# Hybrid MLA and RWKV-7 trunk: eight block copies per inversion move from VectorE to GpSimd

## Chip, cores and metric

The kernel runs on one core of one Trainium2 chip. The metric is device time in microseconds, the median of several executions, lower being better. Every profile is one execution recorded by the hardware profiler; TensorE (PE) is the matrix engine, VectorE (DVE), ScalarE (ACT) and GpSimd (POOL) are the elementwise engines, and SyncE (SP) issues the DMAs.

## What is computed

A decoder trunk of two layers on a sequence of 1024 tokens, model width 1024, in float32. Layer 0 mixes the tokens by latent attention (12 heads), layer 1 by the RWKV-7 recurrence (24 heads of 64); each layer also has four heads of attention to a memory of 256 tokens, a SiLU gate and an output projection. The change lies in layer 1, whose recurrence is, for every head,

```
def step(state, inp):
    r_t, w_t, k_t, v_t, kk_t, a_t = inp
    sa = jnp.einsum('bhvk,bhk->bhv', state, -kk_t)
    state = (state * w_t[:, :, None, :]
             + sa[..., None] * (kk_t * a_t)[:, :, None, :]
             + v_t[..., None] * k_t[:, :, None, :])
    return state, jnp.einsum('bhvk,bhk->bhv', state, r_t)
```

The kernel does not run this token by token. It cuts the 1024 steps into chunks of 64 and solves the dependence inside a chunk with the inverse of a unit triangular 64x64 matrix for each chunk and head.

## The kernel before, in words

**Large products.** Every projection is an fp32 product done as three passes of rounded halves (`mm3`, L160 to L162). Its weights are loaded by SP (L151), rounded by ACT (`wh`, L152), and the remainder is taken by DVE (`wl`, L153, a subtraction of two SBUF operands). PE alternates these products with the small products of the recurrence.

**Layer 1 as a pipeline.** The work is 24 items: 12 pairs of heads times 2 halves of the sequence. An item goes through five stages, one stage per step, so that in each step five items are in flight: `project` (L871), `prep` (L976), `invert` (L1109), `scan` (L1191) and `norm` (L1248). The function `interleave` (L62) mixes the generators of one step; output projections, gates and the memory heads are added to some of the steps.

**The stage `invert`.** For one item it inverts sixteen 64x64 triangular matrices (8 chunks, 2 heads). Both 32x32 diagonal blocks are inverted on DVE by 31 pairs of instructions (L1136 a product into `tmp`, L1140 an addition into `U`, both with two SBUF operands). PE transposes the result into PSUM (L1148), ACT copies it into `inv` as `Uc[0]` and `Uc[1]` (L1152, four copies of 32x256). Then come the lines of the change. DVE makes `X1`, the 32x32 transposes of `Uc[0]` (L1156). Four DVE copies (L1158, 32x128 each) put the blocks of `Uc[1]` on the diagonal of `U2`, and four more (L1165, 32x256 each) put the two diagonal blocks into `XT`. PE multiplies the lower block with `X1` (L1171), ACT takes the result to `M1` (L1180), PE multiplies `M1` with `U2` (L1185), and ACT writes the off-diagonal block into `XT` (L1188). `U2` is one tile for all items, there are two `XT` tiles.

**Who uses the result.** `scan` of that item, in the next step, goes through the eight chunks. For each, DVE masks a product (`gm`, L1216), PE applies the inverse (L1218, reads `XT`), DVE copies the result (L1219), PE forms the state update (L1221) and the output (L1225), and DVE adds up the new state (L1233). The stage `prep` of the item behind has the only regular GpSimd work of layer 1, two memsets of 64x512 per item (L1066).

**What sets the order.** Every engine works through its own queue in order. The order inside a queue is fixed when the program is built: a planner of the tile framework goes by the program's order, by its own model of durations and by which buffers are free. So the queue's order need not be the program's: in some items `X1` stands after the copies on DVE although the program has it first. The tiles `X1`, `M1`, `inv` and most others come from one ring of 54 buffers of 128x512.

Of the kernel before, what the change touches and what calls it, by code (L numbers as in the profile page):

```python
# [71 lines left out]
class Build:  # L72
# [1036 lines left out]
    def invert(self, d, env):  # L1109

        XT, U2, inv, sysd = (d[x] for x in ("XT", "U2", "inv", "sysd"))
        A21 = inv[0:32]
        ip, b_tile = env["ip"], env["b_tile"]
        nc = self.nc
        mm = nc.tensor.matmul
        V, G, ACT = nc.vector, nc.gpsimd, nc.scalar
        As = ip.tile([P, 32, 32], F32, tag="As", name=self.name("As"))
        nc.sync.dma_start(
            As[:].rearrange("p a b -> p (a b)"),
            sysd[:].rearrange("b s r t -> (b s) (r t)").unsqueeze(1).broadcast_to([32, 4, 1024]),  # L1120
        )
        U = ip.tile([P, 32, 8], F32, tag="U", name=self.name("U"))
        tmp = ip.tile([P, 32, 8], F32, tag="tmp", name=self.name("tmp"))
        E = V
        if d["hf"] == 1:
            c0 = self.smp.tile([P, P], F32, tag="c0", bufs=2, name=self.name("c0"))
            nc.sync.dma_start(c0[:], self.carry[d["p"]][:])
            ACT.activation(c0[:], c0[:], AF.Copy, scale=d["f"][:, 8:9])
            d["c0"] = c0[:]
        nc.sync.dma_start(U[:].rearrange("p a b -> p (a b)"), self.A["cst"][:, CU : CU + 256])  # L1130
        for u in range(31, 0, -1):
            if u % 4 == 0:
                yield
            i0 = u // 4
            n = 8 - i0
            E.tensor_tensor(  # L1136
                out=tmp[:, 0:u, 0:n], in0=As[:, 0:u, u : u + 1].broadcast_to([P, u, n]),
                in1=U[:, u : u + 1, i0:8].broadcast_to([P, u, n]), op=ALU.mult,
            )
            E.tensor_tensor(out=U[:, 0:u, i0:8], in0=U[:, 0:u, i0:8], in1=tmp[:, 0:u, 0:n], op=ALU.add)  # L1140
        yield

        Uc = [inv[32:64], inv[64:96]]
        for ih in range(2):
            yield
            ps = b_tile()
            for i in range(4):
                nc.tensor.transpose(ps[0:32, i * P : i * P + P], U[:, :, ih * 4 + i], self.ident)  # L1148
            for b in range(2):
                src = ps[0:32, :].rearrange("p (i s c) -> p i s c", i=4, c=4)[:, :, b * 16 : b * 16 + 16, :]  # L1150
                dst = Uc[b][:, :, ih * 16 : ih * 16 + 16].rearrange("p s (i c) -> p i s c", c=4)
                ACT.copy(dst, src)  # L1152
        yield

        X1 = self.g([32, 16, 32], s="X1")
        V.transpose(X1[:].rearrange("p a b -> p (a b)"), Uc[0].rearrange("p a b -> p (a b)"))  # L1156
        for q in range(4):
            V.tensor_copy(  # L1158
                U2[32 * q : 32 * q + 32, :, 32 * q : 32 * q + 32],
                Uc[1].rearrange("p (g q) t -> p g q t", q=4)[:, :, q, :],  # L1160
            )
        for hd in range(2):
            r0 = hd * 64
            for b in range(2):
                V.tensor_copy(  # L1165
                    XT[r0 + 32 * b : r0 + 32 * b + 32, 0:8, 32 * b : 32 * b + 32],
                    Uc[b].rearrange("p (c h) t -> p c h t", h=2)[:, :, hd, :],
                )
        ps = b_tile()
        for g4 in range(4):  # L1170
            mm(  # L1171
                ps[:, g4 * P : g4 * P + P],
                A21[:, 4 * g4 : 4 * g4 + 4, :].rearrange("p s t -> p (s t)"),
                X1[:, 4 * g4 : 4 * g4 + 4, :].rearrange("p s t -> p (s t)"),
                start=True, stop=True,
            )
        yield
        M1 = self.g([P, 4, 32], s="M1")
        for q in range(4):
            ACT.copy(  # L1180
                M1[32 * q : 32 * q + 32], ps[32 * q : 32 * q + 32, :].rearrange("p (g f) -> p g f", f=P)[:, :, 32 * q : 32 * q + 32]
            )
        ps = b_tile()
        for g4 in range(4):
            mm(ps[0:32, g4 * P : g4 * P + P], M1[:, g4, :], U2[:, g4, :], start=True, stop=True)  # L1185
        for hd in range(2):
            src = ps[0:32, :].rearrange("p (c h t) -> p c h t", h=2, t=32)
            ACT.copy(XT[hd * 64 : hd * 64 + 32, 0:8, 32:64], src[:, :, hd, :])  # L1188
# [187 lines left out]
```

## Time and profile before

| | |
|---|---|
| median of 3 runs | 2519.84 us (2515.22 to 2521.16) |
| the profiled execution | 2510.56 us |
| its span | 2508.8 us |
| mean granted TensorE clock | 0.996 |
| PE busy | 2420.2 us (96%) |
| DVE busy | 1936.4 us (77%) |
| ACT busy | 1375.7 us (55%) |
| POOL busy | 55.1 us (2%) |

The busy time of PE comes from modelled ends of pipelined products. Line numbers (L1165) are those of the kernel printed above. "Idle before" is the time for which an engine had nothing running ahead of the instruction, and the name behind the arrow is what ended it. The first inversion's blocks are ready near 1099 us and the last one's near 2413 us, so that everything the change touches lies between these two times.

### The profile page before, as it was taken

How to read it: one execution, taken by the hardware profiler on the slowest of the kernel's cores; microseconds unless marked ns; L12 is line 12 of the kernel's file. 1: busy time of each engine (PE TensorE's matmuls, PEld its weight loads, DVE VectorE, ACT ScalarE, POOL GpSimd, SP SyncE). 2: the span in 40 equal slices, each digit the busy share in tenths (PEclk: the TensorE clock that was granted, in tenths of full speed). 3: DMA queues.
4: the chain of work that ended last, by engine and by line, in shares of the span. 5: the costliest groups of instructions: out<-in, count | busy, mean ns of one | idle time of the engine just before them, and what ended most of it. 6: DMA issues, size and time to landing. Idle time of an engine off the chain costs nothing.

```text
span 2508.8 us, 39875 instructions
## 1 busy us (share of the span) xinstructions
PE 2420.2 (96%) x13298; PEld 1996.1 (80%) x13298; DVE 1936.4 (77%) x5750; ACT 1375.7 (55%) x2973; POOL 55.1 (2%) x158
## 2 busy tenths in 40 slices
PE   8899999999999999999999999999999999999997
PEld 6698888888888778877778777777777777788785
DVE  7756455877787766698888888888888898786975
ACT  6445345554555334565665666666666665654542
POOL 0000000000000100000000000000000000000000
PEclk9999999999999999999999999999999999999998
DMA  5352222111112443422122222322222123222332
GB/s 178 111 171 85 76 80 74 51 56 54 49 64 68 159 168 136 143 78 76 58 73 79 80 79 78 100 82 77 79 81 80 62 84 118 87 94 98 118 137 70
DMA packets 165982, 231.45 MB, mean 92 GB/s; under 512 B 46096, under 2 KB 67984, under 8 KB 165776
## 3 DMA queue, kind: packets, MB, share of 16 engines
q1 hardware_dynamic: 165776, 228.90, 27.7%
q8 instruction: 105, 1.72, 0.3%
q14 instruction: 101, 0.83, 0.1%
HBM read 187.66 MB, written 37.49 MB: 90 GB/s over the span
## 4 chain that ended last, share of the span: by engine, by line
PE 75%; DVE 15%; ACT 6%; issue 3%; DMA 2%; SPq 0%; DVEq 0%; ACTq 0%
PE mm L160 15%; PE mm L161 15%; PE mm L162 15%; PE a L1085 3%; PE c L1218 2%; DVE tmp L1136 2%; PE pt L724 2%; DVE U L1140 2%; PE c L1221 1%; PE y L1225 1%; PE po L160 1%; PE po L161 1%; PE y L1224 1%; DVE wl L153 1%; PE po L162 1%
## 5 line engine op out<-in xcount | busy, mean ns | idle before, releaser
L152 ACT CAST wh<-wr 128x512 fp32r<-128x512 f32 (+3 forms) x500 | 299.0, 600 | 436.0 <-PE mm L161 381.0
L153 DVE TENSOR_TENSOR wl<-wr,wh 128x512 fp32r<-128x512 f32 (+3 forms) x500 | 329.6, 661 | 132.3 <-ACT wh L152 113.0
L160 PE MATMUL mm<-xnh,wh 128*128 128x512 f32 x912 | 373.9, 410 | 0.8 <-DVE qml L134 0.6
L161 PE MATMUL mm<-xnl,wh 128*128 128x512 f32 x912 | 371.2, 407 | 0.0
L162 PE MATMUL mm<-xnh,wl 128*128 128x512 f32 x912 | 369.7, 406 | 0.0
L160 PE MATMUL mm<-yh,wh 128*128 128x512 f32 x492 | 198.9, 404 | 4.3 <-DVE xr L389 4.1
L162 PE MATMUL mm<-yh,wl 128*128 128x512 f32 x492 | 196.8, 400 | 0.0
L160 PEld LDWEIGHTS mm<-xnh,wh 128*128 128x128 f32 x912 | 172.1, 189 | 30.5 <-issue 2.6
L161 PE MATMUL mm<-yl,wh 128*128 128x512 f32 x492 | 195.5, 397 | 0.0
L161 PEld LDWEIGHTS mm<-xnl,wh 128*128 128x128 f32 x912 | 172.3, 189 | 27.2 <-issue 1.4
L162 PEld LDWEIGHTS mm<-xnh,wl 128*128 128x128 f32 x912 | 172.1, 189 | 27.3 <-issue 1.0
L160 PE MATMUL mm<-xh,wh 128*128 128x512 f32 x416 | 165.2, 398 | 7.6 <-ACT xh L438 7.6
L161 PE MATMUL mm<-xl,wh 128*128 128x512 f32 x416 | 164.9, 396 | 0.6 <-DVE xl L439 0.6
L1140 DVE TENSOR_TENSOR U<-U,tmp 128x60 f32<-128x60 f32 (+24 forms) x744 | 155.9, 210 | 12.3 <-PE b L1171 0.5
L1136 DVE TENSOR_TENSOR tmp<-As,U 128x60 f32<-128x60 f32 (+24 forms) x744 | 155.6, 209 | 12.1
L162 PE MATMUL mm<-xh,wl 128*128 128x512 f32 x416 | 164.3, 395 | 0.0
L1232 ACT ACTIVATE sc<-S,f 128x128 f32<-128x128 f32 x168 | 67.4, 401 | 169.5 <-DVE S L1233 155.9
L302 ACT ACTIVATE p<-b,sm 128x512 f32<-128x512 f32 (+2 forms) x144 | 82.8, 579 | 107.3 <-DVE sm L299 82.2
L389 DVE TENSOR_TENSOR xr<-mm,xr 128x512 f32<-128x512 f32 x123 | 84.5, 688 | 67.1 <-PE mm L162 65.2
L160 PEld LDWEIGHTS mm<-yh,wh 128*128 128x128 f32 x492 | 92.7, 188 | 22.6 <-DVE xr L389 3.5
L297 DVE TENSOR_REDUCE sm<-b 128x1 f32<-128x256 f32 (+1 forms) x176 | 90.3, 527 | 24.8 <-PE b L686 10.1
L162 PEld LDWEIGHTS mm<-yh,wl 128*128 128x128 f32 x492 | 92.7, 188 | 17.0 <-issue 0.2
(361 smaller groups left out, 5968.8 us busy)
## 6 DMA issues: line engine op xcount, KB each, us to landing
wr<-in_wu_dram SPq DMA_DIRECT2D x292, 256.0 KB, 2.7
wr<-in_wo_dram SPq DMA_DIRECT2D x122, 256.0 KB, 2.6
yr<-y SPq DMA_DIRECT2D x60, 256.0 KB, 3.8
As<-sysd SPq DMA_DIRECT2D x24, 512.0 KB, 4.3
y<-y SPq DMA_DIRECT2D x32, 256.0 KB, 2.0
y<-sg SPq DMA_DIRECT2D x32, 256.0 KB, 2.0
g<-u SPq DMA_DIRECT2D x24, 256.0 KB, 2.3
gt<-g SPq DMA_DIRECT2D x24, 256.0 KB, 2.8
```

The source lines that it names most:

```text
L152: nc.scalar.copy(hi[:, :n], raw[:, :n])
L153: nc.vector.tensor_sub(lo[:, :n], raw[:, :n], hi[:, :n].bitcast(F32))
L160: mm(ps, a[0], b[0], start=start, stop=False)
L161: mm(ps, a[0], b[1], start=False, stop=False)
L162: mm(ps, a[1], b[0], start=False, stop=stop)
L297: nc.vector.tensor_reduce(sm[:, i : i + 1], ps[:, :own], AX.X, ALU.max, negate=True)
L302: nc.scalar.activation(p[:, :own], ps[:, :own], AF.Exp, bias=sm[:, 0:1], accum_out=sm[:, 2 + i : 3 + i])
L389: nc.vector.tensor_add(xs[m][:], ps[:], xs[m][:])
L1085: mm(ps[:, j * 256 : j * 256 + 256], BK[c // 4][:, c % 4, :], AR[:, c, :], start=True, stop=True)
L1136: E.tensor_tensor(out=tmp[:, 0:u, 0:n], in0=As[:, 0:u, u : u + 1].broadcast_to([P, u, n]), in1=U[:, u : u + 1, i0:8].broadcast_to([P, u, n ...
L1140: E.tensor_tensor(out=U[:, 0:u, i0:8], in0=U[:, 0:u, i0:8], in1=tmp[:, 0:u, 0:n], op=ALU.add)
L1232: ACT.activation(sc[:], cur, AF.Copy, scale=fc)
```

## The change

The four copies into `U2` and the four into `XT` are issued on GpSimd; operands, shapes and program order stay the same. `X1`, the two products and the ACT copies are as before.

```
@@ -1155,14 +1155,14 @@
         X1 = self.g([32, 16, 32], s="X1")
         V.transpose(X1[:].rearrange("p a b -> p (a b)"), Uc[0].rearrange("p a b -> p (a b)"))
         for q in range(4):
-            V.tensor_copy(
+            G.tensor_copy(
                 U2[32 * q : 32 * q + 32, :, 32 * q : 32 * q + 32],
                 Uc[1].rearrange("p (g q) t -> p g q t", q=4)[:, :, q, :],
             )
         for hd in range(2):
             r0 = hd * 64
             for b in range(2):
-                V.tensor_copy(
+                G.tensor_copy(
                     XT[r0 + 32 * b : r0 + 32 * b + 32, 0:8, 32 * b : 32 * b + 32],
                     Uc[b].rearrange("p (c h) t -> p c h t", h=2)[:, :, hd, :],
                 )
```

## Rows read from the trace of the kernel before

**Rows 1.** The page: busy time of each engine, and the chain that ended last.

```profile
PE 2420.2 (96%) x13298; PEld 1996.1 (80%) x13298; DVE 1936.4 (77%) x5750; ACT 1375.7 (55%) x2973; POOL 55.1 (2%) x158
...
PE 75%; DVE 15%; ACT 6%; issue 3%; DMA 2%; SPq 0%; DVEq 0%; ACTq 0%
```

**Rows 2.** Busy time of each engine by stretch, in layer 1.

```profile
core 0: us, PE busy (x) PEld busy (x) DVE busy (x) ACT busy (x) POOL busy (x), PEclk, DMA share, GB/s
...
1160.00:1770.00 610.00, 589.97 (x3301) 479.14 (x3300) 520.57 (x1815) 382.56 (x841) 10.26 (x20) 1.00 0.25 80
1770.00:2420.00 650.00, 630.78 (x3510) 513.56 (x3509) 547.33 (x1884) 383.51 (x846) 10.41 (x20) 1.00 0.29 96
```

**Rows 3.** Groups by line on DVE, 1100 to 2420: busy us, mean ns | idle before.

```profile
L1165 DVE COPY XT<-inv 32x256 f32<-32x256 f32 x96 | 27.6, 287 | 7.6 <-ACT inv L1152 6.1
...
L1158 DVE COPY U<-inv 32x128 f32<-32x128 f32 x96 | 20.9, 218 | 1.8
L1156 DVE STREAM_TRANSPOSE X<-inv 32x512 f32<-32x512 f32 x24 | 16.8, 700 | 10.7 <-ACT inv L1152 10.2
```

**Rows 4.** Groups by line on PE, 1100 to 2420, same columns.

```profile
L1218 PE MATMUL c<-gm,XT 128*128 128x128 f32 x368 | 74.9, 285 | 9.4 <-DVE gm L1216 3.7 <-DVE tmp L1136 2.6 <-DVE m L193 1.8
...
L334 PE MATMUL a<-cst,mp 128*128 128x128 f32 x64 | 12.0, 282 | 3.5 <-ACT mp L302 3.3
```

**Rows 5.** Timeline of DVE, 1236 to 1244: start, us, instruction [idle before <-releaser].

```profile
1236.81 0.70 DVE L1156 STREAM_TRANSPOSE X<-inv 32x512 f32<-32x512 f32 x1 [1.30 <-ACT inv L1152]
1237.54 0.91 DVE L1158 COPY U<-inv 32x128 f32<-32x128 f32 x4
1238.48 1.18 DVE L1165 COPY XT<-inv 32x256 f32<-32x256 f32 x4
1239.69 0.69 DVE L153 TENSOR_TENSOR wl<-wr,wh 128x512 fp32r<-128x512 f32 x1
...
1243.71 0.28 DVE L1216 TENSOR_TENSOR gm<-c,cst 128x128 f32<-128x128 f32 x1
```

**Rows 6.** Timeline of PE, 1237 to 1245.

```profile
1237.65 1.12 PE L1171 MATMUL b<-X,inv 32*128 32x128 f32 x8 [0.55 <-DVE X L1156]
...
1239.93 1.06 PE L1185 MATMUL b<-U,M 128*32 128x128 f32 x8
...
1244.14 0.46 PE L1218 MATMUL c<-gm,XT 128*128 128x128 f32 x2 [0.64 <-DVE tmp L1136]
```

**Rows 7.** Timeline of DVE, 1779 to 1791, an item in a step with a memory head.

```profile
1779.26 0.58 DVE L1165 COPY XT<-inv 32x256 f32<-32x256 f32 x2 [1.48 <-ACT inv L1152]
...
1781.93 0.45 DVE L1158 COPY U<-inv 32x128 f32<-32x128 f32 x2
1782.39 0.58 DVE L1165 COPY XT<-inv 32x256 f32<-32x256 f32 x2
...
1790.48 0.70 DVE L1156 STREAM_TRANSPOSE X<-inv 32x512 f32<-32x512 f32 x1
```

**Rows 8.** Groups by line on POOL, shapes kept apart: busy us, mean ns | idle before.

```profile
L728 POOL MEMSET pth<- 128x128 f32 x48 | 10.6, 221 | 762.8 <-PE mm L161 397.6 <-PE b L682 134.3 <-PE po L161 69.4
...
L807 POOL MEMSET XT<- 128x576 f32 x2 | 1.4, 717 | 0.0
...
L807 POOL MEMSET U<- 128x512 f32 x1 | 0.5, 524 | 0.0
L552 POOL TENSOR_SCALAR_AFFINE_SELECT msk<-msk 128x128 bf16<-128x128 bf16 x1 | 0.3, 293 | 0.1
```

**Rows 9.** Timeline of POOL at two places.

```profile
1101.51 0.61 POOL L1066 MEMSET SAV<- 64x512 f32 x1 [11.63 <-DMA U<-in_cst_dram]
...
1879.47 0.52 POOL L1066 MEMSET SAV<- 64x512 f32 x1 [32.02 <-PE y L1225]
```

**Rows 10.** Timeline of DVE at the same two places.

```profile
1101.08 1.49 DVE L1165 COPY XT<-inv 32x256 f32<-32x256 f32 x4
...
1879.62 0.68 DVE L1087 TENSOR_TENSOR AM<-a,cst 128x512 f32<-128x512 f32 x1
```

More of the change, by code (lines that the diff above doesn't have):

```diff
@@ L1157, in invert @@
         for q in range(4):
-            V.tensor_copy(
+            G.tensor_copy(
                 U2[32 * q : 32 * q + 32, :, 32 * q : 32 * q + 32],
@@ L1164, in invert @@
             for b in range(2):
-                V.tensor_copy(
+                G.tensor_copy(
                     XT[r0 + 32 * b : r0 + 32 * b + 32, 0:8, 32 * b : 32 * b + 32],
```

## The prediction

> **What bounds the kernel now.** I read the page first: PE is busy for 96% of the span and DVE for 77%, and the chain that ended last is 75% PE and 15% DVE [rows 1]. So the kernel is PE's, with places where PE waits for another engine, and only these places can be gained. The table of stretches says how much they hold where the change works: from 1160 to 2420 us PE is idle for (610 - 590) + (650 - 631) = 39 us of 1260, while DVE is busy for 85% [rows 2]. The groups on PE say which waits stand near the eight copies: 9.4 us ahead of L1218, which waits for DVE's mask `gm`, and 3.5 us ahead of L334 in the memory heads, which waits for ACT's exponential and through it for DVE [rows 4].
>
> The timeline of DVE shows how the copies come into this. An item's `X1` starts as the last block of `inv` arrives, U2's and XT's copies follow, then `wl`, the inversion of the next item, and only at 1243.71 the mask that PE needs at 1244.14, where PE has stood for 0.64 us [rows 5, 6]. This pattern, `X1` first and the copies right behind it, stands in 14 of the 24 items. In nine of them PE waits at L1218 within the next twenty microseconds, for 0.55 to 1.33 us, 7.2 of the 9.4 us. In the other 10 items the copies come early and `X1` three to eleven microseconds after the first of them [rows 7]; seven of these have the wait at L334.
>
> **What goes.** DVE loses 96 copies of 218 ns and 96 of 287 ns, 20.9 + 27.6 = 48.5 us of its busy time [rows 3]. In its queue one item's eight take 1239.69 - 1237.54 = 2.15 us [rows 5]. That is not 24 x 2.15 off the kernel: PE can only take back what it idles. Taken alone, 2.15 us earlier masks cover each of the nine waits whole, 7.2 us. In the rows of the memory heads, a pair of U2's copies and a pair of XT's (0.45 + 0.58 = 1.03 us) stand ahead of the maxima and products of the softmax [rows 7]; that covers the waits at L334, 3.5 us. `X1` and with it L1171 gain nothing: `X1` is ahead of the copies and waits for ACT [rows 3, 5]. The full prize is 10.7 us.
>
> **What comes: the price on POOL.** No row shows a copy on POOL. From below it costs what POOL's memset does: 221 ns for 128 elements, and, by the slope from there to 512 elements, (524 - 221) / 384 = 0.79 ns each, 322 ns for 256 [rows 8]; an item then takes 4 x (0.221 + 0.322) = 2.17 us. A gain below that has no ground, since a copy writes as much as a memset. From above I take rows for larger tiles, 524 ns for U2 and 717 ns for XT, 4.96 us. The nearest row is POOL's one instruction that reads as well as writes, the selection on 128 elements at 293 ns [rows 8]. I take 293 ns for U2's copies and 293 + 128 x 0.79 = 394 ns for XT's: 2.75 us per item, 66 us in all on an engine that is busy for 55 us of 2509 [rows 1].
>
> **What waits for them.** POOL is behind no one: the copies can start with `X1`, as the last ACT block lands. U2 must be ready by L1185, 3.12 us after `X1`'s start [rows 5, 6]; four copies take 1.2 us, at the upper price 2.1. XT must be ready by the next L1218; in the item of the rows that is 7.3 us after `X1`'s start, in the tightest of the 14 it is 5.9 us, against 2.75 (4.96 at the upper price). If that cover were gone, PE would stand at L1185 with the large products queued behind it, one microsecond for one. POOL's queue also holds two memsets per item, which fall tens of microseconds from the copies except in the first item; a memset that starts two microseconds later holds up nobody near it, as the rows it clears are first filled by the scan a step later. No DMA is issued by what moves, so SP's queue, the weights and the loads of `U` and `As` keep their order. I cost all of this at nothing.
>
> **What comes: POOL beside DVE.** This decides. The four XT copies that ran beside a memset took 1.49 us in place of 1.18, and the memset 0.61 in place of 0.52 [rows 5, 9, 10]: the two held each other up. A two-operand instruction beside a memset took 0.68 us, the time of that shape with POOL quiet [rows 5, 9, 10]. DVE's copies take (287 - 218) / 128 = 0.54 ns per element [rows 3], so they move two elements in the time in which others move about one: two streams in and two out. A memset only writes. What fits is that the engines share DVE's second path into and out of memory: a memset takes the second write path, which a two-operand instruction does not need. A copy on POOL also reads, and the second read path is what `wl`, `tmp` and `U` use for their second operand. Those are what DVE runs after `X1`. So I take it that while POOL copies, DVE's two-operand instructions stand, and the reverse. `X1`, with one operand at 700 ns for 512 elements [rows 3], runs freely and covers 1237.54 - 1236.81 = 0.73 us of the copies. The rest, 2.75 - 0.73 = 2.02 us, DVE loses; it saved 2.15. The net is 0.13 us per item, over nine waits 1.2 us. From the waits at L334 I take half, 1.7 us, since the early copies meet two-operand instructions of the memory head as well. **The sum is 1.2 + 1.7 = 2.9 us, about 3 us less.** Against the profiled execution that is 2510.56 - 3 = 2507.6 us. This execution lies 9.3 us under the median of the runs shown; taken from the median, 2519.84 - 3 gives 2517.
>
> The Trainium skill, "SBUF — State Buffer", section "Who interferes with whom", says that a VectorE instruction with two SBUF inputs contends with a GpSimd instruction that reads SBUF and not with one that only writes. The trace agrees with the second half (0.68 us beside the memset); no run here shows the first. By that rule the sum stays at 3 us; were it not so, it would be 10.7.
>
> **The rivals.**
>
> *Only the fast form collides (22%).* If a POOL copy holds up only DVE's two-stream copies, which is all that a row shows, nothing is lost to it: 7.2 + 3.5 = 10.7 us less, 2509; every wait of the two groups, 12.9, would give 2507. For it: the two-operand row beside the memset. Against it: that memset reads nothing.
>
> *POOL's copies are slow (20%).* At 524 and 717 ns DVE stands for 4.96 - 0.73 = 4.23 us per item where it saved 2.15. The loss of 2.08 us lands at L1218 in the nine items where PE already waits: 19 us more, 2539. In all 14 it would be 29 us, 2549. It decides where eight copies exceed 2.15 + 0.73 = 2.88 us, so my own price lies only just under the point. For it: 32 partitions in strips of 32 elements are a finer pattern than a memset's row. Against it: 293 ns for 128 elements read and written.
>
> The Trainium skill, "GPSIMD Engine Reference", section 3.1, calls GpSimd about half as fast as VectorE on elementwise work; doubling the 218 and 287 ns of DVE gives an estimate of 4.0 us per item and about 10 us more. Its section 4.1 calls one-input work roughly line rate, so that page of the Trainium skill speaks for both sides; no run here shows either.
>
> *The planner's new order (13%).* With DVE 2 us lighter per item the planner can place `X1`, `gm` and `wl` elsewhere. That it does so for small reasons is seen in the 10 items where `X1` went behind the copies [rows 5, 7]. The price is of the size of what stands at L1218, 9.4 us, either way [rows 4].
>
> That the change would not do what it says is no rival: the engine is named in each call.
>
> **How the numbers follow.** The forecast, collision and nearly even exchange, has 45%; its own range runs from 6.4 + 3.5 = 9.9 us less (price from below: 4 x 0.543 - 0.73 = 1.44 lost, 0.71 gained in nine waits) to 6 us more (200 ns more for each U2 copy with its XT copy, 0.8 us per item: 9 x (0.8 - 0.13), and nothing from L334), so 2510 to 2526. A difference of 0.3%, 7.6 us, is about what a measurement can tell from none. Faster by more: most of the first rival (0.18), a corner of the forecast (0.05), a third of the planner's case (0.04), 0.27. Slower by more: most of the slow copies (0.17), a corner of the forecast (0.03), a third of the planner's case (0.04), 0.24. The rest, 0.49, is within. The range reaches from 2507, every wait gone, to 2539, the slow copies in nine items.
>
> **What would show it.** In the changed profile: POOL's L1158 and L1165 near 0.29 and 0.39 us; `wl`, `tmp` or `U` beside them stretched by up to one copy; L1218's idle time near 8 to 9 us and L334's near 2; L1185 with no wait for POOL. Two-operand instructions at their old durations and L1218 near 2 us would prove the first rival; copies of half a microsecond and L1218 over 20 us, the second. I am wrong altogether if PE waits at L1185 for U2, or if the time moves with these waits unchanged.

## The result, and the profile after

The changed kernel takes 2503.53 us (median of 4 runs, 2502.14 to 2504.94) beside 2517.66 us for the kernel before (4 runs, 2515.22 to 2521.16): 14.1 us less, ratio 0.994 with a 95% interval of 0.9924 to 0.9956. The predicted 2517.0 us with its range of 2507 to 2539 did not hold it: the gain is larger than the range allowed. (The median of before that the forecast started from was 2519.84 us; a fourth run moved it by 2.2 us.)

The page of the changed kernel, busy time by engine and the chain that ended last; then its table of stretches (same columns as [rows 2]):

```profile
PE 2422.8 (97%) x13298; PEld 2001.3 (80%) x13298; DVE 1898.4 (76%) x5558; ACT 1373.9 (55%) x2973; POOL 126.6 (5%) x350
...
PE 80%; DVE 10%; ACT 6%; DMA 2%; issue 2%; SPq 0%; DVEq 0%; ACTq 0%
```

```profile
1160.00:1770.00 610.00, 592.08 (x3324) 482.42 (x3323) 508.38 (x1746) 383.88 (x845) 41.32 (x101) 1.00 0.25 80
1770.00:2420.00 650.00, 635.73 (x3530) 519.11 (x3529) 531.77 (x1798) 383.84 (x848) 45.55 (x116) 1.00 0.29 96
```

Beside [rows 1, 2]: DVE's share of the chain falls from 15% to 10%, and PE does 7 us more work in the same 1260 us of layer 1 (592.08 + 635.73 beside 589.97 + 630.78). The span goes from 2508.8 to 2501.7 us; the profiled execution of before, 2510.56 us, lies below all four of its runs shown, so that the profiles show half of the medians' difference.

The changed kernel's groups by line, 1100 to 2420: busy us, mean ns | idle before. First the copies on POOL, then PE's waits that answer to [rows 4], and the second small product.

```profile
L1165 POOL COPY XT<-inv 32x256 f32<-32x256 f32 x96 | 40.1, 417 | 963.5 <-ACT inv L1152 959.7
L1158 POOL COPY U<-inv 32x128 f32<-32x128 f32 x96 | 31.8, 331 | 4.1
```

```profile
L1218 PE MATMUL c<-gm,XT 128*128 128x128 f32 x370 | 74.6, 283 | 4.6 <-DVE gm L1216 1.6 <-DVE m L192 1.1 <-DVE m L193 0.8
...
L1185 PE MATMUL b<-U,M 128*32 128x128 f32 x192 | 25.7, 278 | 2.0 <-POOL SAV L1066 0.3 <-issue 0.2
...
L334 PE MATMUL a<-cst,mp 128*128 128x128 f32 x64 | 12.5, 281 | 3.3 <-ACT mp L302 3.1
```

L1218's idle time is halved (9.4 to 4.6), L334's has hardly moved (3.5 to 3.3), and the copies cost what was predicted plus a stretch. The timelines of POOL and of DVE in the item of [rows 5]:

```profile
1237.67 0.82 POOL L1165 COPY XT<-inv 32x256 f32<-32x256 f32 x2 [30.23 <-ACT inv L1152]
1238.54 1.65 POOL L1158 COPY U<-inv 32x128 f32<-32x128 f32 x4
1240.24 0.85 POOL L1165 COPY XT<-inv 32x256 f32<-32x256 f32 x2
```

```profile
1237.64 0.70 DVE L1156 STREAM_TRANSPOSE X<-inv 32x512 f32<-32x512 f32 x1 [1.30 <-ACT inv L1152]
1238.67 0.70 DVE L153 TENSOR_TENSOR wl<-wr,wh 128x512 fp32r<-128x512 f32 x1 [0.33 <-DMA U<-in_cst_dram]
1239.29 0.29 DVE L1136 TENSOR_TENSOR tmp<-As,U 128x31 f32<-128x31 f32 x1
...
1240.29 0.43 DVE L1140 TENSOR_TENSOR U<-U,tmp 128x30 f32<-128x30 f32 x1
...
1241.19 0.21 DVE L1140 TENSOR_TENSOR U<-U,tmp 128x29 f32<-128x29 f32 x1
```

The collision is there: `tmp` and `U` take 0.29 to 0.43 us beside POOL's copies and 0.21 once these are over. But DVE does not stand until all of POOL's copies are done: it gets an instruction through beside each. And the order of the queues has changed too: this `gm` follows at 1243.80, 6.16 us behind X1's start, beside 6.90 in [rows 5], yet elsewhere masks stand later in DVE's queue than before. So three things had to be parted: DVE's relief, the collision, and the new order of the queues.

### The profile page after: what moved, and what is told of

The parts are those of the page before. It is cut to its first block, busy times and chain, and to the rows that moved or that the text cites. A ratio compares the mean times of both kernels' runs of the same rounds, so it can differ in the third digit from the quotient of the medians.

```text
span 2501.7 us, 39830 instructions
## 1 busy us (share of the span) xinstructions
PE 2422.8 (97%) x13298; PEld 2001.3 (80%) x13298; DVE 1898.4 (76%) x5558; ACT 1373.9 (55%) x2973; POOL 126.6 (5%) x350
## 4 chain that ended last, share of the span: by engine, by line
PE 80%; DVE 10%; ACT 6%; DMA 2%; issue 2%; SPq 0%; DVEq 0%; ACTq 0%
PE mm L160 16%; PE mm L161 16%; PE mm L162 16%; PE a L1085 3%; PE c L1218 2%; PE pt L724 2%; PE c L1221 2%; PE y L1225 1%; PE po L160 1%; PE po L161 1%; PE y L1224 1%; PE c L1212 1%; PE c L1214 1%; ACT yT L1241 1%; PE po L162 1%
## 5 line engine op out<-in xcount | busy, mean ns | idle before, releaser
L1140 DVE TENSOR_TENSOR U<-U,tmp 128x60 f32<-128x60 f32 (+24 forms) x744 | 159.4, 214 | 12.7
```

## Experiments

**Holding the order.** For most runs the program is first planned with the copies on one engine; then every queue's order but that of the copies is imposed on the program that is run, by edges that order instructions and add no wait. The copies themselves are placed by the planner. In the traces of the runs that hold before's order, DVE's 5558 instructions other than the copies and ACT's stand in exactly the order of before; those of replan_dve, and of out_free too, stand in that of the changed kernel. Line numbers shift by a few in these kernels; the names show which group is which (`c<-gm,XT` is L1218, `a<-cst,mp` is L334, `b<-U,M` is L1185).

```
+COPIES, ORDER = 'gpsimd', 'vector'   # hold_pool
-            V.tensor_copy(
+            self.copy(                # issues on COPIES
...
+            for queue in order or ():
+                for a, b in zip(queue, queue[1:]):
+                    tc.add_manual_dep(rest[b], rest[a].name, ... NoSync ...)
```

**hold_pool: the copies on POOL, before's order** (`COPIES, ORDER = 'gpsimd', 'vector'`).

> The eight copies are GpSimd's, every other instruction of every queue keeps the order of the kernel before. The change itself took 14.1 us off. Theory A (DVE's relief: the copies leave DVE's queue, and POOL takes back only a part of what they cost there, some 0.2 us per two-operand instruction beside a copy, 0.7 to 1.0 us per item): 7 to 12 us less than before, L1218's idle time 4 to 6 us. Theory B (the new order of the queues): no more than 4 us less, L1218 at 8 to 9 us, as the prediction had it for a fixed order (3 us less).

**replan_dve: the copies on DVE, the changed kernel's order** (`'vector', 'gpsimd'`).

> The eight copies stay VectorE's, every other instruction of every queue stands in the order of the changed kernel. Theory A: within 4 us of before. Theory B: 8 to 14 us less than before, although DVE still does the copies. If both hold a part, this run and hold_pool add up to about 14 us less.

**out_hold: no copies, before's order** (`'', 'vector'`).

> The eight copies of each item are left out, so that the diagonal blocks of U2 and XT stay zero and that part of the inverse is missing; every queue keeps the order of the kernel before. It shows what DVE's whole relief is worth with nothing on POOL: 10.7 us less by the waits of rows 4 taken whole, up to 12.9. Theory A: 10 to 14 us less, and hold_pool 2 to 4 us behind it (the collision's share). Theory B: the same here, but hold_pool 8 us or more behind it.

**out_free: no copies, the planner's own order** (`'', None`).

> The eight copies of each item are left out as in out_hold, and the planner chooses the order itself. Theory A: within 4 us of out_hold. Theory B: a further 8 us or more apart from out_hold, in either direction.

All four ran beside the same 17 runs of before, median 2516.8 us:

| | us | less than before | ratio, 95% interval |
|---|---|---|---|
| hold_pool | 2497.97 | 18.8 | 0.9927, 0.9914 to 0.9940 |
| replan_dve | 2523.92 | -7.1 | 1.0030, 1.0019 to 1.0042 |
| out_hold | 2500.54 | 16.3 | 0.9940, 0.9926 to 0.9955 |
| out_free | 2505.07 | 11.7 | 0.9954, 0.9940 to 0.9967 |

hold_pool gains more than the change itself, and more than the 7 to 12 us that theory A gave; the new order alone makes the kernel slower. Theory B falls. Theory A is right in sign and too small: out_hold gains more than its 14 us, hold_pool, which was to be 2 to 4 us behind out_hold, is level with it or ahead, and the order, which it put within 4 us, costs 7.1 us in replan_dve and 4.5 in out_free. PE's groups in hold_pool, out_hold and replan_dve, same columns and stretch:

```profile
L1225 PE MATMUL c<-gm,XT 128*128 128x128 f32 x372 | 75.7, 285 | 2.7 <-DVE gm L1223 1.8 <-DVE tmp L1143 0.4 <-DVE m L200 0.3
...
L1192 PE MATMUL b<-U,M 128*32 128x128 f32 x192 | 24.9, 272 | 1.9 <-issue 0.2
...
L341 PE MATMUL a<-cst,mp 128*128 128x128 f32 x64 | 11.9, 281 | 1.0 <-ACT mp L309 0.7
```

```profile
L1225 PE MATMUL c<-gm,XT 128*128 128x128 f32 x372 | 75.4, 284 | 2.2 <-DVE gm L1223 1.9
...
L1192 PE MATMUL b<-U,M 128*32 128x128 f32 x192 | 25.5, 276 | 1.0 <-ACT M L1187 0.2
...
L341 PE MATMUL a<-cst,mp 128*128 128x128 f32 x64 | 11.9, 281 | 0.8 <-ACT mp L309 0.7
```

```profile
L1225 PE MATMUL c<-gm,XT 128*128 128x128 f32 x368 | 74.0, 283 | 11.0 <-DVE gm L1223 3.5 <-DVE tmp L1143 2.1 <-DVE m L200 2.1
...
L341 PE MATMUL a<-cst,mp 128*128 128x128 f32 x64 | 12.5, 281 | 7.8 <-ACT mp L309 7.7
```

At a held order the two waits of [rows 4] fall from 12.9 to 3.7 us with the copies on POOL and to 3.0 with none. In the new order with the copies on DVE they rise to 18.8, and the memory heads' wait more than doubles; that is why the change shows L334 unmoved. One place where the new order costs, as the timelines of DVE in the changed kernel and in hold_pool show:

```profile
1337.68 0.21 DVE L1140 TENSOR_TENSOR U<-U,tmp 128x50 f32<-128x50 f32 x1
...
1339.09 0.68 DVE L1258 TENSOR_REDUCE m<-ys 128x8 f32<-128x512 f32 x1
...
1339.89 0.28 DVE L1216 TENSOR_TENSOR gm<-c,cst 128x128 f32<-128x128 f32 x1
```

```profile
1337.29 0.22 DVE L1147 TENSOR_TENSOR U<-U,tmp 128x50 f32<-128x50 f32 x1
1337.77 0.29 DVE L1223 TENSOR_TENSOR gm<-c,cst 128x128 f32<-128x128 f32 x1 [0.26 <-PE c L1219]
```

In before's order the mask stands right behind this `U`, 0.48 us after its start, 0.26 of it DVE's own wait for PE. In the new order eight instructions of the inversion and of `norm` stand between them, the mask starts 2.21 us after `U`, and PE's next L1218 idles 1.11 us for it.

**What the collision takes from DVE.** The instructions of DVE stand in one order in the kernel before, hold_pool and out_hold, so that the distance from `X1` to the same later instruction compares directly. Item of [rows 5], timelines of DVE in the kernel before (`X1` at 1236.81 stands in [rows 5]), in hold_pool and in out_hold:

```profile
1242.83 0.21 DVE L1136 TENSOR_TENSOR tmp<-As,U 128x52 f32<-128x52 f32 x1
```

```profile
1236.90 0.70 DVE L1163 STREAM_TRANSPOSE X<-inv 32x512 f32<-32x512 f32 x1 [1.30 <-ACT inv L1159]
...
1239.05 0.22 DVE L1143 TENSOR_TENSOR tmp<-As,U 128x31 f32<-128x31 f32 x1 [0.43 <-DMA U<-in_cst_dram]
...
1241.94 0.22 DVE L1143 TENSOR_TENSOR tmp<-As,U 128x52 f32<-128x52 f32 x1
```

```profile
1234.47 0.70 DVE L1163 STREAM_TRANSPOSE X<-inv 32x512 f32<-32x512 f32 x1 [1.30 <-ACT inv L1159]
...
1238.60 0.22 DVE L1143 TENSOR_TENSOR tmp<-As,U 128x52 f32<-128x52 f32 x1
...
1240.49 0.29 DVE L1223 TENSOR_TENSOR gm<-c,cst 128x128 f32<-128x128 f32 x1 [0.93 <-PE c L1219]
```

6.02, 5.04 and 4.13 us: without any copies DVE is 1.89 us earlier, with POOL's beside it 0.98. Over the 14 items with `X1` first, the same instruction (the twelfth behind `X1`, copies not counted) comes 1.20 us earlier in out_hold and 0.77 in hold_pool on the mean, 0.43 us apart. Not all of this is the collision. In the item shown, 0.43 us is the wait of the first `tmp` for the DMA that loads `U`; on the mean over the 14, 0.13 us is idle time of DVE, and 0.30 us is the stretch of its instructions. By the pages of the two profiles, DVE's same 5558 instructions are busy for 1890.5 us in out_hold and 1895.9 in hold_pool: beside all 24 items' copies the stretch comes to 5.4 us. And that costs PE nothing that can be seen: in out_hold the mask then waits 0.93 us for PE, and hold_pool is no slower than out_hold, nor the changed kernel (14.1 us less than before) than out_free (11.7), which has its order.

The same load of `U` keeps the saving at 1.20 us, where DVE's queue is rid of 2.15. The groups of `tmp` on DVE, 1100 to 2420, in the kernel before and in out_hold:

```profile
L1136 DVE TENSOR_TENSOR tmp<-As,U 128x60 f32<-128x60 f32 (+24 forms) x713 | 149.1, 209 | 11.5
```

```profile
L1143 DVE TENSOR_TENSOR tmp<-As,U 128x60 f32<-128x60 f32 (+24 forms) x713 | 149.1, 209 | 22.8 <-DMA U<-in_cst_dram 11.7 <-DVE S L1240 0.3
```

With the copies gone DVE reaches the next inversion before its `U` has landed, and idles 11.7 us there in all, a wait that the kernel before does not have.

**pool_x3: more of the collision.**

```
+        for _ in range(REPEAT * (self.copies == "gpsimd")):   # REPEAT = 2
+            for q in range(4):
+                self.copy(inv[96:128, 4 * q : 4 * q + 4], Uc[1]...[:, :, q, :])
+            for hd in range(2):
+                for b in range(2):
+                    self.copy(inv[96:128, 8 * b : 8 * b + 8], Uc[b]...[:, :, hd, :])
```

> hold_pool with each item's eight GpSimd copies done twice more into a part of inv that nobody reads: 16 more copies, 4 x 2 x (0.293 + 0.394) = 5.5 us more of GpSimd's work per item, beside VectorE's chain of tmp and U. If VectorE's two-operand instructions stood for the whole length of a copy (the prediction's step), VectorE loses about 5.5 us more in each of the 14 items: 40 us or more behind hold_pool. If the two take turns, instruction by instruction (some 0.2 us lost per two-operand instruction beside a copy), VectorE loses about 16 x 0.2 = 3.2 us more per item, of which 1 us is still slack: 20 to 30 us behind hold_pool. If GpSimd gives way: within 4 us of hold_pool.

2529.45 us beside 2518.4 for before (9 runs): ratio 1.005, 1.0035 to 1.0065, some 30 us behind hold_pool, each beside before on its own chip. That is at the edge of what taking turns was to cost, and below the 40 us or more of DVE standing. Its group on PE (here to 2440), POOL's extra copies in one row, the first long one of them by itself, and the timeline of DVE beside them:

```profile
L1232 PE MATMUL c<-gm,XT 128*128 128x128 f32 x370 | 75.5, 286 | 12.7 <-DVE gm L1230 6.3 <-DVE m L201 3.0 <-DVE m L204 1.6
```

```profile
1247.94 4.24 POOL L99 COPY inv<-inv 32x128 f32<-32x128 f32 x13
```

```profile
1249.01 0.40 POOL L99 COPY inv<-inv 32x256 f32<-32x256 f32 x1
```

```profile
1248.10 0.21 DVE L1144 TENSOR_TENSOR tmp<-As,U 128x29 f32<-128x29 f32 x1
1248.34 0.21 DVE L1148 TENSOR_TENSOR U<-U,tmp 128x29 f32<-128x29 f32 x1
...
1249.08 0.39 DVE L1144 TENSOR_TENSOR tmp<-As,U 128x54 f32<-128x54 f32 x1
1249.51 0.43 DVE L1148 TENSOR_TENSOR U<-U,tmp 128x54 f32<-128x54 f32 x1
1249.97 0.41 DVE L1144 TENSOR_TENSOR tmp<-As,U 128x52 f32<-128x52 f32 x1
...
1250.88 0.21 DVE L1144 TENSOR_TENSOR tmp<-As,U 128x50 f32<-128x50 f32 x1
...
1251.25 0.28 DVE L1230 TENSOR_TENSOR gm<-c,cst 128x128 f32<-128x128 f32 x1
```

POOL runs without a break here: four extra copies of 32x128 begin at 1247.94, four of 32x256 at 1249.01, four of 32x128 at 1250.71. DVE does one instruction per copy. Beside the short ones, which follow each other every 0.24 us, it keeps its own pace of 0.25 us and loses nothing; beside the long ones, every 0.45 us, its pace is 0.44. So a long copy costs DVE 0.19 us, not its own 0.40. (U2's own short copies follow each other every 0.33 us, and `tmp` and `U` beside them take 0.29 to 0.31: these do cost, some 0.08 us each.) `gm`, whose product lies in PSUM, so that only one of its operands is in SBUF, keeps its 0.28 us beside the copies.

DVE's busy time, for the same instructions, is 1924.4 us beside hold_pool's 1895.9: 28.5 us, 1.2 us per item. Had DVE stood for the 16 extra copies it would be 5.5 us per item. PE's idle time is 16.8 us longer than in hold_pool's profile, 10 of them at L1218 (2.7 to 12.7), and its busy time 11.6 us, at a mean granted clock of 0.993 beside 0.995.

**hold_u2 and hold_xt: one half alone.** Only L1158, or only L1165, on GpSimd, in before's order.

> Only the four copies into U2 are GpSimd's, the four into XT stay VectorE's; the order of before is kept. hold_pool took 18 us off. If a wait is gone as soon as the mask comes about 0.7 us earlier, half the relief (0.9 us per item) gives most of it: 9 to 14 us less. If the gain is proportional to the relief: 18 x 0.91 / 2.15, 8 us less. If GpSimd's copies beside VectorE's fast copies cost both, 5 us less or none.

> Only the four copies into XT are GpSimd's, the four into U2 stay VectorE's; the order of before is kept. Saturating waits: 11 to 16 us less, so that this run and hold_u2 add up to more than hold_pool's 18. Proportional to the relief: 18 x 1.18 / 2.15, 10 us less.

2502.70 us (0.9939, 0.9926 to 0.9952) and 2504.67 us (0.9950, 0.9937 to 0.9963) beside 2518.4: 15.7 and 13.7 us less. Together they are 29, more than hold_pool's 18.8: the waits saturate, and either half gives most of the gain; hold_u2 gains more than the 9 to 14 us that saturation was to give. That the smaller relief gains no less fits the price of the long copies, but the two intervals overlap.

**hold_act: ScalarE in place of GpSimd**, in before's order.

> The eight copies are ScalarE's, the order of before is kept for all else. By ScalarE's copies of these shapes (257 and 362 ns) an item's eight take 2.5 us. If VectorE's relief is all that counts, 15 to 18 us less as in out_hold and hold_pool. If ScalarE's queue, which holds M1 and the blocks between the two small products, is as tight as VectorE's, the copies delay M1 by up to 1 us and later blocks by 2.5 us: between 5 us less and 10 us more than before.

A miss: 2565.45 us, 1.0186 (1.0168 to 1.0203), 47 us slower, far over the 10 that I allowed. Its groups on PE (to 2470):

```profile
L1228 PE MATMUL c<-gm,XT 128*128 128x128 f32 x368 | 74.5, 284 | 2.3 <-DVE gm L1226 1.9
...
L1195 PE MATMUL b<-U,M 128*32 128x128 f32 x184 | 28.3, 304 | 23.8 <-ACT M L1190 23.4
...
L168 PE MATMUL a<-mks,qmh 128*128 128x256 f32 x32 | 10.0, 352 | 11.8 <-ACT mp L310 10.8 <-ACT mks L136 0.6
```

DVE's waits are gone as in out_hold, but PE now waits for `M1`, which stands behind the copies on ACT, 23.8 us in place of hold_pool's 1.9, and 11.8 us in the memory heads, where before waits 1.3. The granted clock fell as well, to 0.98 in both stretches of [rows 2], where before has 1.00:

```profile
1160.00:1770.00 610.00, 574.92 (x3155) 466.33 (x3154) 479.62 (x1666) 393.14 (x886) 10.77 (x21) 0.98 0.25 77
```

PE is busy for 2444.6 us, 24.4 more than before; how the 47 us divide between the waits and the clock was not measured. An engine that is busy for 55% was no free engine at this place.

**after_again and hold_pool_again: both on one chip.**

> The changed kernel as it is, beside hold_pool on one chip. If the planner's new order costs what replan_dve and out_free showed for it (7 and 4.5 us), it comes 4 to 7 us behind hold_pool and 12 to 14 us ahead of before. If hold_pool's lead was a difference of chips: within 2 us of it.

> The copies on GpSimd in the order of before, as in hold_pool: 17 to 19 us less than before, 4 to 7 us ahead of the changed kernel, if the order is what parts them.

2504.06 us (0.9952, 0.9937 to 0.9966) and 2499.71 us (0.9937, 0.9925 to 0.9949) beside 2515.67: 11.6 and 16.0 us less, 4.4 apart. Both gain a little less than expected (12 to 14 and 17 to 19). The intervals overlap, but the three pairs agree in sign: the new order costs 4.4 us with the copies on POOL, 4.5 without copies, 7.1 with them on DVE. hold_pool is the fastest version found.

## Why the prediction was wrong

**The failed step is the term for POOL beside DVE.** "While POOL copies, DVE's two-operand instructions stand, and the reverse", and so 2.02 us lost of 2.15 saved, 0.13 net per item. The measured loss is 0.43 us, of which 0.30 is the collision, and the net 0.77. That the two collide was right; that their times add was wrong. If they added, a pair of `tmp` and a long copy would take 0.25 + 0.45 = 0.70 us; it takes 0.44.

The ends of the instructions show how. The `tmp` at 1249.08 in pool_x3 ends 0.07 us behind the long copy of 1249.01; all 248 stretched `tmp` and `U` of the changed kernel, hold_pool and pool_x3 end 0.06 to 0.09 us behind the copy that they met. Against `wl` it is POOL that waits. In the changed kernel the U2 copy that met `wl` (1238.67 to 1239.37) took 654 ns, beside a median of 289 ns, and ended 0.15 us behind it, while `wl` took 0.70 us and 0.69 in [rows 5] (where it met long copies `wl` was held too, up to 0.92 us in hold_pool):

```profile
1238.87 0.65 POOL L1158 COPY U<-inv 32x128 f32<-32x128 f32 x1
```

All 26 copies that were held up so in the changed kernel end 0.15 us (U2) or 0.25 to 0.26 us (XT) behind the instruction of DVE. So each side does stand until the other is done. But what it has left then, an estimate from these rows, is 0.07 of `tmp`'s 0.21 us, 0.15 of the U2 copy's 0.29, 0.26 of the XT copy's 0.40: some 0.14 us of each pass beside the other engine's work. The prediction charged DVE with the copies' whole time, and did not count that POOL, for which PE hardly waits, bears a part of it.

The Trainium skill, "SBUF — State Buffer", section "Who interferes with whom", says that an instruction with two SBUF inputs contends with a GpSimd instruction that reads; the rows of `tmp` and `U` at 0.39 to 0.43 us now show it. The section "Summary: rules for kernel authors" of that page of the Trainium skill says that the second of the two to issue fully blocks until the first finishes. The ends above agree; read as a price, whole duration upon whole duration, as the prediction in effect did, it gives the 0.70 us where 0.44 was measured.

**The saving** was 1.20 in place of 2.15 us. The prediction put the loads of `U` at nothing, as they keep their order; but with no copies at all DVE waits 11.7 us in all for `U` to land, and `wl` still starts 0.33 us behind `X1`'s end.

**A row misread.** The 0.68 us "beside a memset" is `AM` (L1087), whose `a` lies in PSUM; it has one operand in SBUF, not two. Beside the same memset, from 1879.47 for 0.52 us, stands a row that has two, at its usual time, so that the conclusion holds:

```profile
1879.49 0.21 DVE L1140 TENSOR_TENSOR U<-U,tmp 128x60 f32<-128x60 f32 x1
```

**POOL's price** was right: 293 and 394 ns predicted; undisturbed beside `X1`, two of XT's took 0.82 us with the gaps, the medians are 289 and 396 ns, and the means of 331 and 417 ns hold the stretch. The rival "POOL's copies are slow" was wrong, and with it the upper end of 2539.

**The cover behind POOL** held nearly: L1185 idles 1.9 us in hold_pool beside 1.0 in out_hold, so 0.9 us was paid there that the prediction put at nothing.

**The prize** was about right as idle time of PE and too small as time of the kernel. The waits of [rows 4] gave 10.7 us; at a held order these two groups fall by 9.2 us in hold_pool and L1171, which was to gain nothing, by 1.1 (4.5 in before's profile, 3.4 in hold_pool's), while the runs give 16 to 19. The profiled pair shows 14.0 us (2508.8 to 2494.8): 11.0 of PE's idle time and 3.0 of its busy time (2420.2 to 2417.2), the cause of which is not shown. The rest goes with the granted clock of before's other runs: among runs of one mean clock, 0.995, before takes 2511.60 to 2515.50 and hold_pool 2496.62 to 2500.06, about 14 us apart; but before's 17 runs reach down to 0.991 and hold_pool's six beside them stay at 0.995 and 0.996. That the waits are what pulled the clock down in before's slower runs is an argument, not shown.

**The planner's new order** was a rival of its own, priced at 9.4 us either way. It came in addition, against the gain, at 4 to 7 us. That the planner places things elsewhere when DVE is lighter was right: out_free, with no copies on any engine, has the changed kernel's order on DVE and ACT. What in the planner's model leads to it was not tried.

**"Only the fast form collides"** came near in size, 10.7 us less, for a reason that falls: the two-operand form does collide. It loses little, and what it loses does not show in the time: hold_pool is no slower than out_hold.

## What to carry to other kernels

Where two engines contend, do not cancel a saving against the sum of their busy times: look for how long an instruction still takes once the other engine is done, and which of the two engines has slack to stand. A relief is worth what the next wait leaves of it; here the load of `U` came next. A wait needs only as much relief as it is long, so that half of a move can give most of its gain. A change of engine also changes a planned order: hold the order to learn what the move is worth, and then see whether the held order is the better kernel, as it was here.

## Unexpected of the hardware

Four 32x128 copies on POOL, one after the other, left DVE's chain of 0.21 us two-operand instructions at full pace (0.25 us each, the rows of pool_x3), while 32x256 copies slowed it to 0.44. U2's copies, of the same size but 0.33 us apart, did stretch it (0.29 to 0.31), so that the size alone does not decide.

The time of one kernel's executions goes with the mean granted clock: before's slowest of 17 runs, 2522.81 us, had 0.991, and its one run at 0.996 took 2512.78. In out_hold's profile the clock falls once in layer 1, as its windows (columns of [rows 2]) and its timeline of PE show:

```profile
1620.00:1625.00 5.00, 3.07 (x18) 2.27 (x18) 4.82 (x11) 2.78 (x7) 0.00 (x0) 0.96 0.00 0
1625.00:1630.00 5.00, 4.40 (x23) 3.56 (x22) 4.07 (x12) 3.17 (x7) 0.00 (x0) 0.70 0.07 22
```

```profile
1624.33 1.86 PE L1046 MATMUL a<-rk,cst 128*128 128x512 f32 x2 [1.38 <-DVE rk L1028]
```

PE had been busy for 3.07 of 5 us and had just waited 1.38 us for DVE; then the granted clock means 0.70, between the levels of 2.4 and 1.2 GHz, and the two products behind the wait take 1.01 and 1.06 us, where their group's median is 0.59. hold_pool has the same order and shows no such fall in layer 1, though its PE was busy for only 3.33 of the 5 us from 1625, at a clock of 1.00; the profiled execution of before shows none there either. So a wait of PE can be followed by a lower clock and then cost more than its own length, but not every wait is; how much of hold_pool's gain came that way was not measured by itself.
